# Wide tiles read as four rows of 2048 bytes instead of 2112 in an encoder block on one core

## The chip, the core and the metric

The kernel runs on one core of a Trainium2 chip. A core has five engines that each work through a stream of instructions of their own: TensorE (PE: matmuls; PEld: the loads of its stationary operand), VectorE (DVE), ScalarE (ACT), GpSimd (POOL) and SyncE (SP), with 16 DMA engines beside them. Its on-chip memory has 128 partitions, and matmul results land in eight PSUM banks of 128 x 512 f32. The metric is the device time of one execution in microseconds (us); lower is better.

## The reference

One layer of an encoder, f32, 512 positions of width 1024: a SwiGLU block, a mixer (a gated convolution beside a bidirectional chunked mLSTM with four heads), and a second SwiGLU block, each between two RMS norms.

```python
def swiglu(x, w_in, w_out):                   # w_in 1024 x 5632, w_out 2816 x 1024
    gate, up = jnp.split(x @ w_in, 2, axis=-1)
    return (jax.nn.silu(gate) * up) @ w_out
...
        h = swiglu(rmsnorm(x, norm_ffn1_pre[l]), w_ffn1_in[l], w_ffn1_out[l])
        x = x + FFN_RESIDUAL_SCALE * rmsnorm(h, norm_ffn1_post[l])
        h = mixer(rmsnorm(x, norm_mix_pre[l]), w_mix_in[l], conv_w[l], conv_b[l],
                  gate_i_bias[l], gate_f_bias[l], mlstm_norm[l], w_mix_out[l])
        x = x + rmsnorm(h, norm_mix_post[l])
        h = swiglu(rmsnorm(x, norm_ffn2_pre[l]), w_ffn2_in[l], w_ffn2_out[l])
        x = x + FFN_RESIDUAL_SCALE * rmsnorm(h, norm_ffn2_post[l])
```

## The kernel before

**Products in two halves.** Each large product is made of fp32r operands. `split` (L362) takes an f32 tile and makes `hi`, its fp32r copy (ScalarE, L363), and `lo`, the remainder (VectorE, L366). A product then is three matmuls or three runs of matmuls into one PSUM bank: hi times hi, hi times lo, lo times hi. Weights are read from HBM into `raw` tiles, split into `whi` and `wlo`, and most products are arranged as seven products of half-size blocks instead of eight (`combine_x`, `w_pair`, `left_a`, `left_b`, `product_out`), whose sums and differences VectorE forms.

**Wide tiles.** The pool `big` has 13 buffers of 128 partitions x 4 rows x `BW` = 528 numbers, that is 8448 bytes of a partition, in rows 2112 bytes apart. Nearly all users fill 512 numbers (2048 bytes) of a row and leave 64 bytes. Two users fill rows of 528: the weights of v with their 16 columns of gates behind 512 columns (`v_split`, L892), and `vaug` (L935), which holds v for four heads of 132 numbers a row. The others are the following.

- The normed and transposed input of a product, `xq_tile` (L402): one tile of hi and one of lo for each group of four rows of 128 features. These are the moving operands of `mm_cols` (L507, whole rows of 512 columns), of `mm_part` (L516, halves of a row, 256 columns), and of `plain` (L542, the same).
- `h`, the result of the first product of a SwiGLU block (L527), six tiles, a row for each 128 hidden features.
- `hs` (L767): in rows q and q+1 the hi and the lo of a row of `h`. They are the stationary operand of `mm_out` (L745), in blocks of 128 columns.
- `ea`, `eb`, `xb` (L706): intermediate sums of 512 columns.
- In the mixer: keys, queries, gates, convolution results, and the result tiles whose blocks are the stationary operand of the output projection (L1425); `RA`, `RB`, `HLT`, `QT` (L966 to L982) for the log-gate sums.
- As one flat run, not as rows: `halves` (L583), whose 256- or 512-wide pieces are the operands of `product_out` (L723), and the output weights of the mixer, `wmo` (L1407). Their pieces start at multiples of 512 bytes from the tile's start.

The innermost loops of the two forms that read rows as moving operands are these:

```python
        for ww, xx in ((0, "h"), (0, "l"), (1, "h")):
            for k in range(KD):
                nc.tensor.matmul(
                    o, w[ww][:, k, :], xq_tile(xq, (k // 4, xx))[:, k % 4, FULL], start=n == 0, stop=n == 3 * KD - 1)
...
        for ww, xx in ((hi, 0), (hi, 1), (lo, 0)):
            for k in range(4):
                pin(nc.tensor.matmul(
                    o, ww[:, k, :], x[xx][:, k, :], start=first and n == 0, stop=n == 11, skip_group_check=True))
```

**Stages.** The program runs, in us of the profiled execution: loads and first norm (0 to 26), the first product of the first SwiGLU block (26 to 257, L542 and L516), its second product (257 to 320, L723 and L745) and the norm behind it (to 344), the product for v and the gates (344 to 370, L950), the mixer (370 to 505, L507 and the recurrence), its output projection (505 to 548, L1425), and the second SwiGLU block in the same stages (548 to 858), with the last norms and the stores (to 887).

**Order.** A scheduler orders the instructions of each engine; instructions that pass through `pin` keep the order in which the code issues them, and `tc.issue_after` puts others behind a marked one. The big weights come over SP's DMA queue, some of them over POOL's. A tile of the pool `big` is given to a new user when its last reader is done.

Of the kernel before, what the change touches and what calls it, by code (L numbers as in the profile page):

```python
# [8 lines left out]
F32 = mybir.dt.float32  # L9
F32R = mybir.dt.float32r  # L10
# [6 lines left out]
P = 128  # L17
# [19 lines left out]
BW = 528  # L37
# [4 lines left out]
def encoder_kernel(ctx: ExitStack, tc: tile.TileContext, a: dict, out: bass.AP):  # L42
# [4 lines left out]
    big = ctx.enter_context(tc.tile_pool(name="big", bufs=13))  # L47
# [11 lines left out]
    def nm(s):  # L59
        uid[0] += 1  # L60
        return f"{s}_{uid[0]}"

    def bigt(dt=F32):
        return big.tile([P, 4, BW], dt, tag="big", name=nm("big"))

    def ps():
        return psum.tile([P, 512], F32, tag="ps", name=nm("ps"))
# [10 lines left out]
    def f32(ap):  # L78
        return ap.bitcast(F32)

    def blk(i, n=P):
        return slice(i * n, (i + 1) * n)

    def ch(v):
        return v.rearrange("p (c t) -> p c t", t=P)
# [211 lines left out]
    def w_get(ahead=2):  # L297
        w_split(max(0, 1 + ahead - len(ready)))
        return ready.pop(0)
# [62 lines left out]
    def split(hi, lo, src, eng=nc.vector):  # L362
        latest["hi"] = nc.scalar.copy(out=hi, in_=src)  # L363
        if pinned["act"]:
            pin(latest["hi"])
        latest["lo"] = eng.tensor_tensor(out=lo, in0=src, in1=f32(hi), op=ALU.subtract)  # L366
        pin(latest["lo"])
# [34 lines left out]
    def xq_tile(xq, key):  # L402
        if key not in xq["q"]:
            xq["q"][key] = bigt(F32R)
        return xq["q"][key]
# [7 lines left out]
    def flip_q(tb, xs, xq, halves=(0, 1), bank=None):  # L413

        full = []
        for b in halves:
            pt = bank or ps()
            for k in range(4):
                pin(nc.tensor.transpose(out=pt[:, blk(k)], in_=xs[:, blk(4 * b + k)], identity=ident))  # L419
            hi, lo = xq_hl(xq, (b, tb // 2))  # L420
            split(hi[:, :, blk(tb % 2)], lo[:, :, blk(tb % 2)], ch(pt))
            if b not in xq["f"]:
                xq["f"][b] = bigt()
            if bank:
                return lambda fn: pin(fn(xq["f"][b][:, :, blk(tb)], ch(pt)))
            full.append((b, pt))
        for b, pt in full:
            pin(nc.scalar.copy(xq["f"][b][:, :, blk(tb)], ch(pt)))
# [91 lines left out]
    def ffn(xq, between, finish, mid=None, within=None, ahead=(2, 2, 1, 1), late=None, prep=None, block=0):  # L520
# [4 lines left out]


        h = [bigt() for _ in range((NF + 3) // 4)]  # L527
        spare.extend(h[-1][:, q, 0:512] for q in (2, 3))

# [362 lines left out]
    def v_split():  # L892
        for i in range(4):
            if not loaded:
                w_load(1)
            (raw,), _ = loaded.pop(0)
            bt = bigt(F32R).rearrange("p q f -> p (q f)")
            hi, lo = (bt[:, blk(n, 2 * BW)].rearrange("p (k f) -> p k f", k=2) for n in range(2))
            split(hi[:, :, 0:512], lo[:, :, 0:512], raw.rearrange("p (k f) -> p k f", k=2))
            rg = rawg[:, 2 * i:2 * i + 2, :]  # L900
            nc.gpsimd.tensor_copy(out=hi[:, :, 512:BW], in_=rg)
            nc.gpsimd.tensor_tensor(out=lo[:, :, 512:BW], in0=rg, in1=f32(hi[:, :, 512:BW]), op=ALU.subtract)
            wv.append((hi, lo))
# [14 lines left out]
    def within1(tb):  # L918
        if tb >= 2:
# [6 lines left out]
            (2, 1): lambda: flip_q(2, st1[2], xT1), (3, 0): lambda: mark.update(latest), (3, 1): lambda: flip_q(3, st1[3], xT1),  # L926
        },
        finish1, wgates, within1, (1, 1, 1, 0), late1, v_split)
    xq = st["xq"]

# [1 line left out]
        return xq_hl(xq, (k // 4, tb // 2))[hl][:, k % 4, blk(tb % 2)]  # L932


    vaug = bigt()  # L935
    vv = vaug.rearrange("p c (h e) -> p c h e", e=BW // 4)
    nc.gpsimd.memset(vv[:, :, :, DV:DV + 1], 1.0)
    spread = t2()
# [26 lines left out]
    with tc.issue_after(mark["pow"].ins):  # L965
        RA, RB = bigt(), bigt()  # L966
        nc.gpsimd.memset(RA[0:36, 0:2], 0.0)
        I, F = RA[0:36, 0, 0:512], RA[0:36, 1, 0:512]
        T1, T2 = RA[0:36, 2, 0:512], RA[0:36, 3, 0:512]
        B, A = RB[0:36, 0, 0:512], RB[0:36, 1, 0:512]  # L970
        CM, U = RB[0:36, 2, 0:512], RB[0:36, 3, 0:512]
        nc.gpsimd.memset(U, 1.0)
        nc.gpsimd.memset(ch(U)[:, :, 0:1], 0.0)
        HLT = bigt(F32R)
        UHL, IHL = HLT[:, 0, 0:512], HLT[:, 1, 0:512]
        nc.gpsimd.memset(f32(HLT[:, 0:2]), 0.0)
        sel = HLT.rearrange("p q f -> p (q f)")[:, 2 * BW:2 * BW + 8 * P].rearrange("p (j m) -> p j m", m=P)
        QT = bigt()
        Q1, Q2 = QT[:, 0, 0:512], QT[0:36, 1, 0:512]
        nc.gpsimd.memset(QT[:, 0:2], 0.0)  # L980
        parl = QT[0:36, 2, 0:2 * DK]
        nc.gpsimd.tensor_copy(parl.rearrange("p (e x) -> p e x", x=DK), par.broadcast_to([36, 2, DK]))  # L982
        gm = const.tile([36, 4, 8], F32, name="gm")
        amax, gsum, mprev, aco = gm[:, 0, 0:4], gm[:, 1, 0:4], gm[:, 2, :], gm[:, 3, 0:4]
        nc.vector.memset(mprev[:, 0:1], NEG)
# [261 lines left out]
        pn2[:, 256:272], parl, acd.rearrange("p q c -> p (q c)"),  # L1247
        start=True, stop=True,
    )
    Ct = bigt()  # L1250
    Cf = Ct.rearrange("p q f -> p (q f)")
    Cs = Cf[:, 0:12 * 129].rearrange("p (q i e) -> p q i e", q=4, i=3)
    nat1 = Cf[:, 1552:2064].rearrange("p (c r) -> p c r", r=P)
# [147 lines left out]
    for n, k in enumerate(MIXK):  # L1401
        if n < 5:
            wmo[k] = w_get(0)
        else:
            raw = rawp.tile([P, 1024], F32, tag="raw", name=nm("raw"))
            nc.sync.dma_start(raw, wo[blk(k), :])
            bt = bigt(F32R).rearrange("p q f -> p (q f)")  # L1407
            split(bt[:, 0:1024], bt[:, 1024:2048], raw)
            wmo[k] = (bt[:, 0:1024], bt[:, 1024:2048])
    for tb in range(NT):  # L1410
# [58 lines left out]
```

## Time and profile before

| | |
|---|---|
| time, median of 3 runs | 888.0 us (886.79 to 888.97) |
| the profiled execution | 888.25 us |
| its span | 886.5 us |
| mean granted TensorE clock | 0.999 |
| PE busy | 875.6 us, 99% of the span, 6039 instructions |
| PEld busy | 807.4 us, 91% |
| DVE busy | 731.8 us, 83%, 1159 instructions |
| ACT busy | 491.8 us, 55%, 855 instructions |
| POOL busy | 93.7 us, 11%, 123 instructions |
| DMA | 123.24 MB, 139 GB/s over the span |

The span runs from the first to the last instruction that the profiler recorded; the execution takes 1.75 us more. Matmuls overlap in the pipeline, so their single durations (280 ns for a 128x256 one of L516) add up to more than their time, and the distance from one matmul to the next is the better measure. A row of the groups reads: line, engine, operation, result<-operands by the program's names, shapes, count, then busy time in us, mean ns of one, and the engine's idle time ahead of them with what ended it. A row of the chain reads: start and length in us, engine, tile, line and count of a piece in which the instructions follow each other on one engine. A row of the windows reads: the stretch, its length, then the busy time and count of each engine, the granted clock, the DMA engines' mean share and the GB/s moved.

### The profile page before, as it was taken

Reading aid. Unit: us, or ns where it says so; the run is one execution under the profiler, and the core shown is the slowest. Engines: PE = TensorE matmul, PEld = TensorE weight load, DVE = VectorE, ACT = ScalarE, POOL = GpSimd, SP = SyncE. Lnnn points to the kernel's source line nnn. Section 1 sums busy time; section 2 is a strip of 40 time slices with the busy share of each in tenths; the row PEclk is TensorE's granted clock in tenths of the full one; section 3 lists DMA queues with packets and bytes.
Section 4 is the critical chain, followed back from the end, with each engine's and each line's share of the span. In section 5 each row is a group of like instructions: output and inputs, shape, how many; then the busy total and the mean of one; then the engine's idle time right before and its main releaser. Section 6 shows DMA issues by size and latency. Waiting matters only on the chain.

```text
span 886.5 us, 15403 instructions
## 1 busy us (share of the span) xinstructions
PE 875.6 (99%) x6039; PEld 807.4 (91%) x6039; DVE 731.8 (83%) x1159; ACT 491.8 (55%) x855; POOL 93.7 (11%) x123
## 2 busy tenths in 40 slices
PE   8999999999999999999999999999999999999997
PEld 6999999999988889988988888999999999988885
DVE  6989898988889978887588757898898988869956
ACT  7656455544656645755565535654555555546722
POOL 5000000001132022100121011000000000223000
PEclk9999999999999999999999999999999999999999
DMA  8444433424998852442062733433333423899722
GB/s 255 126 120 121 118 94 98 118 84 129 216 261 201 278 181 83 121 118 71 1 190 91 213 111 102 128 105 108 96 96 96 132 83 105 201 243 231 267 72 95
DMA packets 140384, 123.24 MB, mean 139 GB/s; under 512 B 5500, under 2 KB 116112, under 8 KB 140312
## 3 DMA queue, kind: packets, MB, share of 16 engines
q1 hardware_dynamic: 129936, 97.62, 36.8%
q0 software_dynamic: 10368, 24.65, 12.5%
q8 instruction: 47, 0.77, 0.3%
q14 instruction: 25, 0.20, 0.1%
q10 hardware_dynamic: 8, 0.01, 0.0%
HBM read 115.96 MB, written 6.29 MB: 138 GB/s over the span
## 4 chain that ended last, share of the span: by engine, by line
PE 96%; DMA 1%; DVE 1%; issue 0%; ACT 0%; DVEq 0%; POOLq 0%; POOL 0%; ACTq 0%
PE ps L516 47%; PE ps L723 19%; PE ps L507 9%; PE ps L542 5%; PE ps L1425 5%; PE ps L745 5%; PE ps L950 3%; DMA raw<-in_w_mix_in_dram 1%; PE ps L419 1%; PE ps L1328 1%; DMA g_row<-in_norm_ffn_pre_dram 1%; PE ps L472 0%; PE ps L1336 0%; PE ps L1277 0%; DVE t L464 0%
## 5 line engine op out<-in xcount | busy, mean ns | idle before, releaser
L516 PE MATMUL ps<-big,whi 128*128 128x256 f32 x2064 | 283.8, 280 | 0.4 <-DVE t L1086 0.4
L516 PEld LDWEIGHTS ps<-big,whi 128*128 128x128 f32 x2064 | 261.0, 188 | 1.9 <-DVE t L1086 0.8
L363 ACT CAST whi<-raw 128x1024 fp32r<-128x1024 f32 x170 | 175.5, 1051 | 72.6 <-DVE raw L216 23.6
L366 DVE TENSOR_TENSOR wlo<-raw,whi 128x1024 fp32r<-128x1024 f32 x166 | 201.3, 1220 | 13.0 <-ACT whi L363 8.7
L516 PE MATMUL ps<-big,wlo 128*128 128x256 f32 x1032 | 161.6, 280 | 0.0
L516 PEld LDWEIGHTS ps<-big,wlo 128*128 128x128 f32 x1032 | 138.8, 188 | 0.0
L723 PE MATMUL ps<-whi,big 128*128 128x512 f32 x336 | 105.7, 389 | 0.0
L723 PEld LDWEIGHTS ps<-whi,big 128*128 128x128 f32 x336 | 62.9, 188 | 13.0
L516 PE MATMUL ps<-big,ws 128*128 128x256 f32 x516 | 69.9, 280 | 0.0
L170 POOL DMA_DIRECT2D raw<-in_w_ffn_out_dram x18 | 22.0, 1221 | 440.6 <-DMA raw<-in_w_ffn_out_dram 222.5
L723 PE MATMUL ps<-wlo,big 128*128 128x512 f32 x168 | 64.8, 389 | 0.0
L516 PEld LDWEIGHTS ps<-big,ws 128*128 128x128 f32 x516 | 64.7, 188 | 0.0
L690 ACT COPY t<-ps 128x256 f32<-128x256 f32 x40 | 14.9, 373 | 88.4 <-PE ps L516 88.4
L507 PE MATMUL ps<-big,whi 128*128 128x512 f32 x224 | 55.2, 397 | 0.0
L507 PEld LDWEIGHTS ps<-big,whi 128*128 128x128 f32 x224 | 41.4, 188 | 9.3
L363 ACT CAST whi<-t 128x1024 fp32r<-128x1024 f32 (+1 forms) x44 | 39.5, 913 | 15.3 <-DVE t L216 10.2
L366 DVE TENSOR_TENSOR wlo<-t,whi 128x1024 fp32r<-128x1024 f32 (+1 forms) x44 | 46.2, 1051 | 1.4 <-ACT whi L363 0.7
L745 PE MATMUL ps<-whi,big 128*128 128x512 f32 x128 | 40.3, 393 | 0.0
L723 PEld LDWEIGHTS ps<-wlo,big 128*128 128x128 f32 x168 | 31.5, 188 | 6.5
L692 DVE TENSOR_TENSOR t<-ps,t 128x256 f32<-128x256 f32 x40 | 16.9, 423 | 20.7 <-PE ps L516 20.5
L542 PE MATMUL ps<-big,whi 128*128 128x256 f32 x256 | 33.8, 283 | 0.0
L542 PEld LDWEIGHTS ps<-big,whi 128*128 128x128 f32 x256 | 31.7, 188 | 0.6 <-ACT big L363 0.3
(245 smaller groups left out, 1408.0 us busy)
## 6 DMA issues: line engine op xcount, KB each, us to landing
raw<-in_w_ffn_in_dram SPq DMA_DIRECT2D x68, 512.0 KB, 4.6
raw<-in_w_ffn_out_dram SPq DMA_DIRECT2D x26, 512.0 KB, 4.7
raw<-in_w_mix_in_dram SPq DMA_DIRECT2D x24, 512.0 KB, 4.7
t<-in_w_ffn_in_dram SPq DMA_DIRECT2D x20, 512.0 KB, 3.7
raw<-in_w_ffn_out_dram SPq DMA_DIRECT2D x36, 256.0 KB, 6.2
raw<-in_w_ffn_out_dram POOLq DMA_DIRECT2D x18, 512.0 KB, 7.8
xd<-x POOLq DMA_DIRECT2D x8, 512.0 KB, 2.9
x<-xd POOLq DMA_DIRECT2D x8, 512.0 KB, 5.2
```

What stands on the lines that cost most here:

```text
L170: nc.gpsimd.dma_start(sums.rearrange("p (g f) -> p g f", g=2), top[:, 512:1024].rearrange("p (g f) -> p g f", g=1).broadcast_to([P, 2, 512 ...
L363: latest["hi"] = nc.scalar.copy(out=hi, in_=src)
L366: latest["lo"] = eng.tensor_tensor(out=lo, in0=src, in1=f32(hi), op=ALU.subtract)
L507: nc.tensor.matmul(o, w[ww][:, k, :], xq_tile(xq, (k // 4, xx))[:, k % 4, FULL], start=n == 0, stop=n == 3 * KD - 1)
L516: pin(nc.tensor.matmul(o, ww[:, k, :], x[xx][:, k, :], start=first and n == 0, stop=n == 11, skip_group_check=True))
L542: pin(nc.tensor.matmul(o, ww[:, k, :], xq_hl(xq, (k // 4, th))[xx][:, k % 4, :], start=n == 0, stop=n == 3 * KD - 1))
L690: nc.scalar.copy(a_[:, h1], x[:, h0])
L692: nc.vector.tensor_tensor(out=c[:, h1], in0=y[:, h0], in1=a_[:, h1], op=ALU.add)
L723: nc.tensor.matmul(acc[tb + t][half], left[n][x][:, blk(t)], right[n][y], start=first and x == y == 0, stop=last_ and x == 1, skip_group_c ...
L745: nc.tensor.matmul(acc[tb][half], hT[hh][:, blk(tb)], w[ww][:, blk(half, 512)], start=fresh and hh == ww == 0, stop=k == NF - 1 and hh == ...
L950: nc.tensor.matmul(pv_[i][:, 0:at.stop - at.start], xv(xx, k, tb), ww[:, k % 2, at], start=n == 0, stop=n == 3 * KD - 1)
L1425: nc.tensor.matmul(acc[half], yy[yi][:, k % 4, blk(tb)], wmo[k][wi][:, blk(half, 512)], start=(n == 0 and yi == 0 and wi == 0), stop=(n == ...
```

## The change

A new helper `wide()` makes the tile as it was, 128 x 2112 numbers. `bigt()` now takes its first 2048 numbers and reads them as four rows of 512, so that rows lie 2048 bytes apart. Where a row needs 528 numbers (`v_split`, `vaug`), or where the tile is used flat past 2048 numbers (`Ct`), the tile is taken from `wide()` as before; `wmo` takes it flat. `sel` starts at the number 8 x 128 = 1024 of `HLT` instead of 2 x 528 = 1056: the start of the third row, as before. The pool, its 13 buffers and their size stay.

```diff
+    def wide(dt=F32):
+        return big.tile([P, 4 * BW], dt, tag="big", name=nm("big"))
+
     def bigt(dt=F32):
-        return big.tile([P, 4, BW], dt, tag="big", name=nm("big"))
+        return wide(dt)[:, 0:2048].rearrange("p (q f) -> p q f", q=4)
...
-            bt = bigt(F32R).rearrange("p q f -> p (q f)")
+            bt = wide(F32R)
             hi, lo = (bt[:, blk(n, 2 * BW)].rearrange("p (k f) -> p k f", k=2) for n in range(2))
...
-    vaug = bigt()
+    vaug = wide().rearrange("p (q f) -> p q f", q=4)
...
         HLT = bigt(F32R)
         UHL, IHL = HLT[:, 0, 0:512], HLT[:, 1, 0:512]
         nc.gpsimd.memset(f32(HLT[:, 0:2]), 0.0)
-        sel = HLT.rearrange("p q f -> p (q f)")[:, 2 * BW:2 * BW + 8 * P].rearrange("p (j m) -> p j m", m=P)
+        sel = HLT.rearrange("p q f -> p (q f)")[:, 8 * P:16 * P].rearrange("p (j m) -> p j m", m=P)
...
-    Ct = bigt()
+    Ct = wide().rearrange("p (q f) -> p q f", q=4)
...
-            bt = bigt(F32R).rearrange("p q f -> p (q f)")
+            bt = wide(F32R)
             split(bt[:, 0:1024], bt[:, 1024:2048], raw)
```

On every engine the instructions are the same in kind, number, order and waits before and after; only addresses differ, and the length of three memsets on POOL, at the place in the mixer where the tiles of the log-gate sums are cleared (`big_4357` is `RA`, `big_4358` is `RB`, `big_4362` is `HLT`, `big_4364` is `QT`). POOL's rows there before:

```order
L967 MEMSET big_4357 36x1056
L972 MEMSET big_4358 36x512
L976 MEMSET big_4362 128x1056
L980 MEMSET big_4364 128x1056
L982 COPY big_4364<-par 36x128
L973 MEMSET big_4358 36x4
```

and POOL's rows there with the change (its lines are three further on):

```order
L970 MEMSET big_4357 36x1024
L975 MEMSET big_4358 36x512
L979 MEMSET big_4362 128x1024
L983 MEMSET big_4364 128x1024
L985 COPY big_4364<-par 36x128
L976 MEMSET big_4358 36x4
```

Nothing has moved; the three memsets over two whole rows no longer cover the 64 bytes at the end of each row.

## The prediction

> **What bounds the kernel now.** I read first the chain of work that ended last, then what TensorE waits for, then the busy time by stage, and last the chain again piece by piece, because a piece of it has a start, a length and a count, and so gives the spacing of the matmuls in it.
>
> ```profile
> span 886.5 us, 15403 instructions
> PE 96%; DMA 1%; DVE 1%; issue 0%; ACT 0%; DVEq 0%; POOLq 0%; POOL 0%; ACTq 0%
> PE ps L419 <- DVE t L464: 2.8, 2, 2.3
> PE ps L353 <- POOL gbias L877: 1.4, 1, 1.4
> PE ps L516 <- DVE t L1086: 0.4, 1, 0.4
> ```
>
> TensorE is 96% of the chain, and in the whole execution it waits 4.6 us for another engine. So almost all of the time is matmuls that stand directly behind each other, and a change counts only through the spacing of matmuls. The stages say how much cover the other engines have:
>
> ```profile
> core 0: us, PE busy (x) PEld busy (x) DVE busy (x) ACT busy (x) POOL busy (x), PEclk, DMA share, GB/s
> 26.00:257.00 231.00, 231.00 (x1873) 227.09 (x1872) 202.80 (x312) 126.56 (x200) 12.88 (x12) 1.00 0.48 130
> 344.00:370.00 26.00, 26.00 (x219) 25.96 (x217) 19.58 (x30) 17.99 (x40) 7.12 (x12) 1.00 0.33 104
> 575.00:796.00 221.00, 221.00 (x1783) 216.84 (x1782) 188.31 (x298) 117.01 (x190) 12.09 (x11) 1.00 0.47 126
> ```
>
> In the two long stretches of 256-wide products VectorE is busy 202.80 of 231 us and 188.31 of 221 us, the DMA engines about half of the time. TensorE can gain some 10% there before another engine is the bound. The granted clock is 1.00 in all three stages, so nothing here hangs on the clock.
>
> **What one matmul costs, by where its operands lie.** The pieces of the chain below are start, length, line and count. Each length divided by its count is the spacing from one matmul to the next.
>
> ```profile
> 37.41 196.29 PE ps L516 x1668
> 237.87 83.00 PE ps L723 x366
> 376.67 27.34 PE ps L507 x118
> 504.14 22.27 PE ps L1425 x96
> 858.13 22.09 PE ps L745 x96
> ```
>
> The last four are all 128x512 matmuls of the same type, yet their spacings are 83.00/366 = 226.8 ns (L723), 27.34/118 = 231.7 (L507), 22.27/96 = 232.0 (L1425) and 22.09/96 = 230.1 (L745). Not even the order within them explains it: L723, L745 and L1425 all take left and right operands in the order hi-hi, hi-lo, lo-hi. What sets L723 apart is its addresses. In the built program the wide tiles start at 24256 + n x 8448 bytes of a partition and the weight tiles at 134080 + n x 4096, and all of these starts lie 192 bytes past a multiple of 256. L723 reads weight tiles and flat halves of wide tiles, in steps of 512, 1024, 2048 and 4096 bytes, so every operand of it keeps that place. L507 streams rows of wide tiles 2112 bytes apart, and 2112 = 8 x 256 + 64: each row begins 64 bytes further on in the 256-byte period. L745 and L1425 load their stationary operand from such rows. With rows of 2048 = 8 x 256 bytes all of them would lie as L723's do. That is the one thing in the profile which this change can move.
>
> The durations of single matmuls say the same as the spacings:
>
> ```profile
> L723 PE MATMUL ps<-whi,big 128*128 128x512 f32 x336 | 105.7, 389 | 0.0
> L507 PE MATMUL ps<-big,whi 128*128 128x512 f32 x224 | 55.2, 397 | 0.0
> L745 PE MATMUL ps<-whi,big 128*128 128x512 f32 x128 | 40.3, 393 | 0.0
> L1425 PE MATMUL ps<-whi,big 128*128 128x512 f32 x80 | 26.4, 394 | 0.0
> L1425 PE MATMUL ps<-big,big 128*128 128x512 f32 x72 | 18.8, 396 | 0.0
> ```
>
> 389 ns stands for L723 in every group, 393 to 397 for the others.
>
> **The change part by part.** The order of instructions, their number and their waits stay as they were on every engine.
>
> *512-wide matmuls.* L507 runs 336 times, L745 192 times, L1425 192 times. If they take L723's spacing, they save 336 x (231.7 - 226.8) = 1.65 us, 192 x (230.1 - 226.8) = 0.63 us and 192 x (232.0 - 226.8) = 1.00 us, together **3.3 us**. All of it is on the chain: these pieces are TensorE behind TensorE. Bounds: nothing, if the addresses are not the cause, and 3.3 us; I take the full 3.3, since L723 is the only group with this layout and holds its spacing over 366 matmuls.
>
> *256-wide matmuls whose moving operand is a wide row.* L516 runs 3612 times and L542 384 times, 3996 together, so each nanosecond of spacing is 4.0 us: this is the large unknown. Now they stand at 196.29/1668 = 117.7 ns, with each moving row 64 bytes further on than the one before. The trace has no 256-wide matmul of this type in the layout to come. The nearest rows:
>
> ```profile
> 106.77 1.22 PE L516 MATMUL ps<-big,ws 128*128 128x256 f32 x9
> 107.83 1.57 PE L516 MATMUL ps<-big,whi 128*128 128x256 f32 x12
> 109.24 0.63 PE L516 MATMUL ps<-big,wlo 128*128 128x256 f32 x4
> ...
> 111.70 0.64 PE L516 MATMUL ps<-big,wlo 128*128 128x256 f32 x4
> 112.18 0.98 PE L516 MATMUL ps<-big,whi 128*128 128x256 f32 x7
> ```
> ```profile
> 344.80 8.75 PE ps L950 x72
> ```
>
> From below: the same saving as at 512 columns, 4.9 ns, gives 112.8 ns and 3996 x 4.9 = 19.6 us. If the saving goes with the columns, it is half of that, 2.45 ns and 9.8 us. From above: runs of four in L516 take between (109.24 - 107.83)/12 = 117.5 ns and (112.18 - 111.70)/4 = 120.0 ns, the slow ones where the scheduler has put another product in between and the 64-byte step is broken; if the slow spacing became the rule, the loss were 2.3 ns and 9.2 us. The nearest row is L950: it runs pairs of 256 and 272 columns over one weight, the second of each pair 1024 bytes after the first, thus with no step in the 256-byte period. Its mean is 8.75/72 = 121.5 ns for a mean of 264 columns; taking off 8 columns at (231.7 - 117.7)/256 = 0.445 ns leaves 117.9 ns, against 117.7 with the step. So I take **0** for the 256-wide matmuls, and keep -19.6 and +9.2 us as ends.
>
> A page of the Trainium skill speaks against any effect: TensorE: Matmul & The Clock Gate, section Back-to-back issue gap, gives the gap of a warm matmul as its columns over 2.4 GHz plus about 2.5 ns, with no address in it. By that rule 512 columns take 215.8 ns and 256 take 109.2 whatever the pitch, and the change is worth nothing. The rows agree only in part: the same shape stands at four spacings here, all of them above the rule's.
>
> *VectorE and ScalarE.* They read and write the same rows, in one to four runs.
>
> ```profile
> L366 DVE TENSOR_TENSOR wlo<-raw,whi 128x1024 fp32r<-128x1024 f32 x166 | 201.3, 1220 | 13.0 <-ACT whi L363 8.7 <-PE ps L723 3.0 <-ACT junk L1362 0.8
> L366 DVE TENSOR_TENSOR big<-t,big 128x1024 fp32r<-128x1024 f32 x6 | 7.3, 1222 | 0.0
> L428 ACT COPY big<-ps 128x512 f32<-128x512 f32 x12 | 6.9, 589 | 2.3 <-DVE big L366 2.1
> L479 ACT COPY raw<-ps 128x512 f32<-128x512 f32 x4 | 2.4, 589 | 2.3 <-DVE big L366 2.2
> ```
>
> A subtraction over one flat run takes 1220 ns, over four runs 2112 bytes apart 1222; a copy into runs 2112 apart takes 589 ns, into runs 1024 apart 589. The pitch costs these engines nothing that can be seen, so I put 0 there, between bounds of plus and minus 2 ns an instruction; even 2 ns on all of them lies under TensorE.
>
> *The three memsets on GpSimd*, which clear two whole rows each, shrink from 1056 to 1024 numbers.
>
> ```profile
> L967 POOL MEMSET big<- 36x1056 f32 x1 | 1.0, 972 | 0.0
> L972 POOL MEMSET big<- 36x512 f32 x1 | 0.5, 517 | 0.0
> ```
>
> That is (972 - 517)/544 = 0.84 ns a number, 27 ns each, 0.08 us in all, on an engine that is busy 7.12 of 26 us in that stage (344 to 370) and that TensorE is not waiting for. It counts 0. The DMAs into wide rows move 512 numbers to a partition before and after.
>
> **The sum.** The profiled execution took 888.25 us, 1.75 us of it around the span of 886.5; it lies 0.25 us above the median of 888.0 of the runs shown. 888.25 - 3.3 = 884.95 for it, and against the median 888.0 - 3.3 = **884.7 us**.
>
> **The rivals.**
>
> *Nothing changes: 888.0 us.* For it: L723 has no fixed spacing either. Its first twelve matmuls, with the same addresses to the 256 bytes, are slow:
>
> ```profile
> 233.70 2.76 PE ps L723 x12
> ```
>
> 2.76/12 = 230.0 ns, as slow as L745. So the slow spacing also comes from something that is not the address, perhaps the change from 256-wide to 512-wide products just before, and L507, L745 and L1425 may be slow for such a reason. Against it: L745 runs 96 in a row at 858.13 without ever becoming fast, L723 becomes fast after its first dozen and stays so.
>
> *The 256-wide matmuls gain too.* Then 888.0 - 3.3 - 9.8 = 874.9 us if the gain goes with the columns, and 888.0 - 3.3 - 19.6 = 865.1 us if each matmul gains the same. For it: their moving rows step by 64 bytes just as L507's do. Against it: L950's spacing above. No other engine would cap it: 1680 matmuls at 4.9 ns take 8.2 us from the stretch of 231 us and leave 222.8, above VectorE's 202.80.
>
> *The 256-wide matmuls lose: slower than before.* The mechanism is the one place: a matmul whose moving row starts at the same place of the 256-byte period as the one before it. In L516 that happens now only where products are interleaved, and runs of four there take up to 120.0 ns. If every one of the 3996 took 120.0 ns, the kernel would take 888.0 - 3.3 + 9.2 = 893.9 us. It decides from 3.3/3996 = 0.8 ns on; from 1.5 ns on the kernel is slower by more than 0.3%. For it: at 512 columns the good layout still costs 226.8 ns where twice 112.8 would be 225.6, so a part of the cost is fixed for each matmul and may be larger than I take it. Against it: L950.
>
> **How the numbers follow.** Chances: my forecast, 512-wide gain alone and the 256-wide within 0.8 ns either way (881.5 to 888), 0.36; nothing changes (887 to 889) 0.22; 256-wide gain (865 to 881.5) 0.24; 256-wide lose (888 to 894) 0.18. About 0.3%, 2.7 us, is what a measurement of this kernel can tell from no change: faster means under 885.3, slower over 890.7. Of the forecast's 0.36, 0.23 lies under 885.3 and 0.13 above. Faster is then 0.23 + 0.24 = 0.47; of the losing case's 0.18, 0.04 lies under 890.7. Same is 0.13 + 0.22 + 0.04 = 0.39, less 0.01 for a case of no change that comes out above 890.7 by the spread of the runs, thus 0.38; slower is 0.14 + 0.01 = 0.15. The range of 8 in 10 leaves out the lower half of the gaining case, 0.12, and the upper end of the losing one, 0.05: **869 to 892 us**. The likeliest case's own range is 881.5 to 888.
>
> **What would show it.** In the profile of the changed kernel, right: the chain's pieces of L507, L745 and L1425 at 226.8 ns, single durations of 389 ns in place of 393 to 397, and L516 at 117.7 +- 0.8 ns over its run of about 1668. VectorE and ScalarE groups keep their means. Wrong: L507 still at 231.7 (then the addresses are not the cause, and L723 is fast for its own reasons), or L516 away from 117.7, which decides the time alone, since 4.0 us hang on each of its nanoseconds. A new wait of TensorE for VectorE in the stretch 26 to 257 would mean that I have misjudged the cover.

## The result and the profile after

The changed kernel takes 893.55 us (median of 6 runs, 892.69 to 894.2) against 887.45 us before (6 runs, 886.79 to 888.97): a ratio of 1.0065, 95% interval 1.0055 to 1.0076. It is 0.65% slower, clear of what a measurement can confuse with no change. The forecast was 884.7 us, the range 869 to 892.

The head of the page of the changed kernel, whose lines are numbered three higher than before:

```profile
span 891.6 us, 15403 instructions
PE 882.6 (99%) x6039; PEld 817.1 (92%) x6039; DVE 731.6 (82%) x1159; ACT 492.2 (55%) x855; POOL 92.2 (10%) x123
```

The span is 5.1 us longer, VectorE and ScalarE are about as busy as before (731.8 and 491.8 there), and TensorE's busy time grew by 7.0 us, while its waits fell by 1.9 us, from 4.6 to the 2.7 shown below. Next the pieces of the changed kernel's chain that answer to those of before (start, length, line, count):

```profile
37.32 200.16 PE ps L519 x1668
241.66 82.99 PE ps L726 x366
380.07 26.78 PE ps L510 x118
506.09 21.79 PE ps L1428 x96
577.67 197.28 PE ps L519 x1644
863.58 21.77 PE ps L748 x96
```

Each piece has the count that it had before, so lengths compare directly. The 512-wide products became faster: `mm_cols` (L510) from 27.34 to 26.78 us, which is 226.9 ns a matmul, the output projection (L1428) from 22.27 to 21.79, 227.0 ns, `mm_out` (L748) from 22.09 to 21.77, 226.8 ns; `product_out` (L726) kept its spacing, 226.8 before and 226.7 now. The 256-wide product `mm_part` (L519) became slower: 196.29 to 200.16 us for 1668 matmuls, 117.7 to 120.0 ns.

What TensorE waits for in the changed kernel, whole answer (engine, line, releaser: us in total, times, longest):

```profile
PE ps L356 <- POOL gbias L880: 1.4, 1, 1.4
PE ps L422 <- DVE t L467: 1.3, 2, 1.1
```

No wait in a product took the place of another: both are in the start of the program. What changed in the products is the spacing of matmuls. 3996 x 2.32 ns = 9.3 us lost, and 336 x 4.75 + 192 x 3.3 + 192 x 5.0 ns = 3.2 us gained, is 6.1 us, the difference of the two medians.

### The profile page after: what moved, and what is told of

It reads as the page before. It is cut to its first block, busy times and chain, and to the rows that moved or that the text cites. A ratio compares the mean times of both kernels' runs of the same rounds, so it can differ in the third digit from the quotient of the medians.

```text
span 891.6 us, 15403 instructions
## 1 busy us (share of the span) xinstructions
PE 882.6 (99%) x6039; PEld 817.1 (92%) x6039; DVE 731.6 (82%) x1159; ACT 492.2 (55%) x855; POOL 92.2 (10%) x123
## 4 chain that ended last, share of the span: by engine, by line
PE 98%; DMA 1%; DVE 0%; ACT 0%; issue 0%; DVEq 0%; POOLq 0%; POOL 0%; SPq 0%; ACTq 0%
PE ps L519 49%; PE ps L726 19%; PE ps L510 9%; PE ps L545 5%; PE ps L1428 5%; PE ps L748 5%; PE ps L953 3%; PE ps L1331 1%; PE ps L422 1%; DMA x<-in_x_dram 1%; PE ps L1339 0%; PE ps L475 0%; PE ps L1280 0%; PE ps L1307 0%; PE ps L1300 0%; PE ps L1373 0%
## 5 line engine op out<-in xcount | busy, mean ns | idle before, releaser
L519 PE MATMUL ps<-big,whi 128*128 128x256 f32 x2064 | 288.6, 283 | 0.0
L519 PEld LDWEIGHTS ps<-big,whi 128*128 128x128 f32 x2064 | 266.2, 192 | 1.1 <-ACT t L1312 0.2
L519 PE MATMUL ps<-big,wlo 128*128 128x256 f32 x1032 | 164.2, 283 | 0.0
L519 PEld LDWEIGHTS ps<-big,wlo 128*128 128x128 f32 x1032 | 141.7, 192 | 0.0
L726 PE MATMUL ps<-whi,big 128*128 128x512 f32 x336 | 105.6, 389 | 0.0
L726 PEld LDWEIGHTS ps<-whi,big 128*128 128x128 f32 x336 | 62.9, 188 | 12.9
L519 PE MATMUL ps<-big,ws 128*128 128x256 f32 x516 | 71.2, 283 | 0.0
L519 PEld LDWEIGHTS ps<-big,ws 128*128 128x128 f32 x516 | 66.0, 192 | 0.0
L726 PE MATMUL ps<-wlo,big 128*128 128x512 f32 x168 | 64.7, 389 | 0.0
L510 PE MATMUL ps<-big,whi 128*128 128x512 f32 x224 | 54.5, 394 | 0.0
L510 PEld LDWEIGHTS ps<-big,whi 128*128 128x128 f32 x224 | 41.4, 188 | 8.7
L748 PE MATMUL ps<-whi,big 128*128 128x512 f32 x128 | 39.8, 390 | 0.0
L726 PEld LDWEIGHTS ps<-wlo,big 128*128 128x128 f32 x168 | 31.6, 188 | 6.5
L545 PE MATMUL ps<-big,whi 128*128 128x256 f32 x256 | 34.2, 285 | 0.0
L545 PEld LDWEIGHTS ps<-big,whi 128*128 128x128 f32 x256 | 32.1, 192 | 0.5 <-ACT big L366 0.3
```

Source lines behind the costliest of these rows:

```text
L510: nc.tensor.matmul(o, w[ww][:, k, :], xq_tile(xq, (k // 4, xx))[:, k % 4, FULL], start=n == 0, stop=n == 3 * KD - 1)
L519: pin(nc.tensor.matmul(o, ww[:, k, :], x[xx][:, k, :], start=first and n == 0, stop=n == 11, skip_group_check=True))
L545: pin(nc.tensor.matmul(o, ww[:, k, :], xq_hl(xq, (k // 4, th))[xx][:, k % 4, :], start=n == 0, stop=n == 3 * KD - 1))
L726: nc.tensor.matmul(acc[tb + t][half], left[n][x][:, blk(t)], right[n][y], start=first and x == y == 0, stop=last_ and x == 1, skip_group_c ...
L748: nc.tensor.matmul(acc[tb][half], hT[hh][:, blk(tb)], w[ww][:, blk(half, 512)], start=fresh and hh == ww == 0, stop=k == NF - 1 and hh == ...
```

## The experiments

Two theories could be had from the result. **The step:** the rival of the prediction, by which a matmul is slow at 256 columns when its moving row starts at the same place of the 256-byte period as the row before it. **The relative place:** what counts is how far the moving row's start lies from the stationary block's start modulo 256 bytes; in the changed kernel both are at byte 192 throughout, whereas before, rows 2112 bytes apart went through all four distances 0, 64, 128 and 192. A third, **the traffic of other engines** at the new pitch, had to be excluded. In the following, *distance* is the start of the moving row less the start of the stationary block, modulo 256 bytes, from the built programs. All matmuls named below have fp32r operands and a stationary block of 128 x 128, and TensorE runs the same 6039 instructions in the same order in every kernel here.

### Moving rows alone back to 2112 bytes (x_2112)

```diff
-    def bigt(dt=F32):
-        return wide(dt)[:, 0:2048].rearrange("p (q f) -> p q f", q=4)
+    def bigt(dt=F32, pitch=512):
+        return wide(dt)[:, 0:4 * pitch].rearrange("p (q f) -> p q f", q=4)
...
-            xq["q"][key] = bigt(F32R)
+            xq["q"][key] = bigt(F32R, 528)
```

> Only the moving rows (the tiles that xq_tile makes, for both SwiGLU blocks and the mixer) go back to rows 2112 bytes apart; all other wide tiles keep 2048. Theory, the step: the spacing of matmuls hangs on whether the moving row starts at the same place of the 256-byte period as the one before it. Then mm_part returns from 120.0 to 117.6 ns, mm_cols from 227 to 231.7, while mm_out and the output projection, whose stationary rows stay at 2048, keep 226.8 and 227.0: 893.55 - 3996 x 2.32 ns + 336 x 4.7 ns = 885.9 us. Rival, the traffic of the other engines: the loss comes from VectorE, ScalarE and DMAs that read and write the wide rows at another pitch while TensorE streams; since most of these rows (h, hs, ea, eb, xb) stay at 2048, mm_part would stay near 120 ns and the time near 893.

Measured: 885.83 us (one run; before on the same chip 887.09). Its chain:

```profile
36.19 196.29 PE ps L519 x1668
375.06 27.34 PE ps L510 x118
502.89 21.79 PE ps L1428 x96
856.02 21.77 PE ps L748 x96
```

The first two pieces have the lengths of the kernel before to the hundredth, the last two those of the changed one. So the pitch of the moving rows sets `mm_part` and `mm_cols`, the pitch of the stationary rows sets `mm_out` and the projection, and the other engines' traffic in `h`, `hs`, `ea`, `eb` and `xb` sets neither. The traffic rival falls for these tiles. What the other engines write into the moving rows themselves went back to the old pitch too; gap64 below, with every row at 2048 bytes, excludes that as well. The step theory and the relative place both fit.

### Only the rows read in halves back to 2112 (x_mix)

With the helper of x_2112:

```diff
-            xq["q"][key] = bigt(F32R)
+            xq["q"][key] = bigt(F32R, 512 if "m" in xq and isinstance(key, tuple) else 528)
```

> Moving rows that are read in halves of 256 columns go back to 2112 bytes (both SwiGLU blocks, and the four tiles of differences in the mixer); the mixer's tiles that are read over 512 columns, and all rows that serve as stationary operand, keep 2048. By the step theory mm_part and plain take 117.6 ns (but for some 108 matmuls of the mixer that share the 512-wide tiles), mm_cols, mm_out and the output projection 226.8 to 227: 893.55 - 3888 x 2.32 ns = 884.5 us, thus under the kernel before (887.45) by 0.3%. By the rival of the other engines' traffic it stays near 893.

Measured: 884.59 us (8 runs) against 887.09, ratio 0.9975 (0.9965 to 0.9986). From its chain:

```profile
36.66 196.29 PE ps L519 x1668
375.56 26.78 PE ps L510 x118
```

`mm_part` has the spacing of the kernel before and `mm_cols` that of the changed one, so the two terms are separate. The time is 2.5 us under the kernel before, where the prediction had forecast 3.3 for the 512-wide term by itself; some 108 matmuls of 256 columns, in the mixer, still had the slow layout here, which by 2.32 ns each is 0.25 us of the rest.

### A step of 32 bytes (x_2080)

Also with the helper of x_2112:

```diff
-            xq["q"][key] = bigt(F32R)
+            xq["q"][key] = bigt(F32R, 520)
```

> All moving rows 2080 bytes apart: a step of 32 bytes instead of 64. If any break of the place in the period counts, mm_part takes 117 to 118 ns and mm_cols 230 to 232: 885.9 us, as with 2112. If the size of the step sets the gain in proportion, mm_part takes 118.8 ns and the time is some 889.7. If only whole 64-byte blocks count, mm_part stays at 120.0 and mm_cols at 227: 893.5.

Measured: 888.93 us (one run; before 887.09). From its chain:

```profile
36.32 197.65 PE ps L519 x1668
376.62 27.24 PE ps L510 x118
```

`mm_part` takes 118.5 ns, `mm_cols` 230.8: between the two layouts, near the line for a gain in proportion (118.8 ns, 889.7 us). By itself this told little. A step of 32 bytes also goes through the four distances 0, 32, 64 and 96 instead of 0, 64, 128 and 192, which is another mean under the second theory.

### Distance 192 without a step (gap64)

```diff
+    gapw = ctx.enter_context(tc.tile_pool(name="gapw", bufs=1))
     wpool = ctx.enter_context(tc.tile_pool(name="wpool", bufs=12))
...
+    gapw.tile([P, 16], F32, name="gapw")
```

> All rows at 2048 as in the changed kernel, but the weight tiles (and the tiles behind them) start 64 bytes later, so that moving rows start at byte 192 and the stationary blocks of mm_part at byte 0 of the 256-byte period, throughout and without any step. Step theory: nothing changes, mm_part 120.0 ns and 893.5 us. Rival, the relative place: the slow spacing comes from both operands starting at the same place of the period, which before happened for a quarter of the matmuls only; then mm_part falls to 117 ns or less, 884 us or less, and mm_out and the output projection leave 226.8.

Measured: 873.42 us (one run; before 887.09). From its chain, whose lines are two higher than the changed kernel's:

```profile
37.33 189.04 PE ps L521 x1668
230.50 83.77 PE ps L728 x366
369.97 27.53 PE ps L512 x118
843.40 21.99 PE ps L750 x96
```

All rows are 2048 bytes apart, there is no step anywhere, and `mm_part` takes 189.04/1668 = 113.3 ns instead of 120.0. The step theory falls: it had said 120.0. At the same time every 512-wide product left its best: `mm_cols` at distance 192 takes 233.3 ns, `product_out` and `mm_out` at distance 64 take 228.9 and 229.1. The sum 3996 x -6.7 + 336 x 6.4 + 756 x 2.2 + 384 x some 2.5 ns is -22.0 us; measured are -20.1. Of the rest, 1.0 us is a wait of the first product for ScalarE, which the changed kernel does not have; the remainder is not worked out.

### The same distance by moving the other operand (at48)

```diff
-    def bigt(dt=F32):
-        return wide(dt)[:, 0:2048].rearrange("p (q f) -> p q f", q=4)
+    def bigt(dt=F32, at=0):
+        return wide(dt)[:, at:at + 2048].rearrange("p (q f) -> p q f", q=4)
...
-            xq["q"][key] = bigt(F32R)
+            xq["q"][key] = bigt(F32R, 0 if "m" in xq and isinstance(key, tuple) else 48)
```

> Weight tiles stay where the changed kernel has them (byte 192 of the 256-byte period). The moving rows that are read in halves of 256 columns start 48 numbers (192 bytes) further into their wide tile, rows 2048 bytes apart: byte 128, thus again 192 bytes behind the stationary blocks modulo 256, as in gap64, but by moving the other operand. The mixer's tiles that are read over 512 columns, and all stationary rows, stay at byte 192, in step with what they meet. Theory, the relative place: mm_part and plain take 113.4 ns, mm_cols 227, mm_out 226.8, product_out 226.8: 893.55 - 3888 x 6.55 ns = 868.1 us, if VectorE keeps up (it was busy 183 of 200 us in the first long stretch of gap64). Rival, the absolute place of the weights (gap64 was fast because the weight tiles began at byte 0): mm_part stays at 120.0 ns, 893.5 us.

Measured: 868.83 us (median of 6 runs, five of them from 868.43 to 869.32 and one of 876.38, for which no cause is known) against 887.22, ratio 0.9809 (0.9783 to 0.9835). Its chain, then what TensorE waits for:

```profile
36.05 189.04 PE ps L519 x1668
229.24 82.96 PE ps L726 x366
367.63 26.78 PE ps L510 x118
564.68 186.32 PE ps L519 x1644
839.52 21.77 PE ps L748 x96
```

```profile
PE ps L356 <- POOL gbias L880: 1.4, 1, 1.4
PE ps L422 <- DVE t L467: 0.9, 2, 0.5
PE ps L519 <- DVE t L1089: 0.8, 1, 0.8
```

The weights are where the changed kernel has them, and `mm_part` takes the 189.04 us of gap64 all the same: the place of the weights alone is not the cause; the distance is what the two kernels share. The 512-wide products keep distance 0 and their best spacing, so this kernel has both gains; it is the fastest of the study, 1.9% under the kernel before and 2.8% under the changed one. VectorE keeps up, as the only wait for it in a product is 0.8 us long.

### Both operands moved together (all0)

```diff
+    gapb = ctx.enter_context(tc.tile_pool(name="gapb", bufs=1))
     big = ctx.enter_context(tc.tile_pool(name="big", bufs=13))
...
+    gapb.tile([P, 16], F32, name="gapb")
```

> The changed kernel with 64 bytes put in ahead of the wide tiles, so that wide tiles and weight tiles both start at byte 0 of the period and their distance is 0 as in the changed kernel. Relative place: mm_part 120.0, mm_cols 227, mm_out 226.8, 893.5 us. Absolute place of either operand: mm_part leaves 120.0, and comes to 113.4 if gap64 was fast through the weights at byte 0.

Measured: 893.85 us (one run; before 887.22). From its chain:

```profile
37.20 200.16 PE ps L521 x1668
241.54 83.22 PE ps L728 x366
380.16 26.80 PE ps L512 x118
863.92 21.77 PE ps L750 x96
```

In `mm_part`, `mm_cols` and `mm_out` both operands start 64 bytes further on, at byte 0, and their pieces are the changed kernel's: 120.0, 227.1 and 226.8 ns. Moving both operands by 64 bytes makes no difference as long as their distance stays. `product_out` alone became slower, 83.22 us against 82.99. 168 of its 756 stationary blocks lie in the tiles `xl`, in a pool ahead of the added 64 bytes, which did not move; their distance is now 64 instead of 0, and a matmul with such a block lasts 391 to 392 ns in this trace, one with another block 389. In gap64, with distance 64 throughout, all of them last 391 to 392 ns.

### The other distances (at16, at32, at40, at56)

The edit is that of at48 with other numbers: 16, 32, 40 and 56 numbers for the rows read in halves, and 32, 48, 8 and 56 for the mixer's rows read over 512 columns.

> As at48, but the rows read in halves start 64 bytes into their tile (64 ahead of the stationary blocks modulo 256) and the mixer's rows read over 512 columns 128 bytes (128 ahead). Relative place: if only the equal place is bad at 256 columns, mm_part takes 113.4 ns and the time is 868 to 870; if the spacing changes with the distance, anything from 113.4 to 123 (the pitch 2080 showed single intervals of up to 124). mm_cols over 512 columns leaves 227 for 229 to 234. Absolute place of the weights: 120.0 and 893.5.

> As at16, with 128 bytes for the rows read in halves and 192 bytes for the mixer's rows read over 512 columns. Relative place: mm_cols takes 233.3 ns, as in gap64 at the same distance; mm_part somewhere between 113.4 and 123, 113.4 if only the equal place is bad. Absolute place of the weights: 120.0 and 227.

> A finer look at the distance: rows read in halves 160 bytes into their tile, the mixer's rows read over 512 columns 32 bytes. The spacings so far over the distance: at 256 columns 120.0 (0), 117.8 (64), 118.7 (128), 113.5 ns (192); at 512 columns 227 (0), 229 (64), 232.6 (128), 233.3 (192). If the spacing moves evenly between these points, mm_part takes 116.1 ns and mm_cols 228: 878.8 us. If only the whole 64-byte block of the start counts, 160 acts as 128 and 32 as 0: mm_part 118.7, mm_cols 227, 889 us; if it is rounded up, 113.5 and 229, 869.5 us.

> Rows read in halves and the mixer's rows read over 512 columns both 224 bytes into their tile. Evenly between the points: mm_part 116.7 ns, mm_cols 230, 882 us. By whole 64-byte blocks: as at 192, mm_part 113.5, mm_cols 233.3, 870.9 us. If the best place lies between 192 and 256: mm_part under 113.4 and the time under 868.

Measured: 886.24 and 889.14 us (one run each, before 887.22) for at16 and at32; 889.53 us (ratio 1.0021, 1.0011 to 1.0031) for at40 and 888.62 us (1.0013, 1.0003 to 1.0022) for at56, both against 887.36. The two pieces of each chain, in this order of kernels:

```profile
36.80 196.45 PE ps L519 x1668
375.84 27.42 PE ps L510 x118
```

```profile
36.41 197.94 PE ps L519 x1668
376.97 27.53 PE ps L510 x118
```

```profile
36.84 197.94 PE ps L519 x1668
377.63 27.54 PE ps L510 x118
```

```profile
37.47 197.38 PE ps L519 x1668
377.67 27.54 PE ps L510 x118
```

Length by count, with the kernels above, gives the spacing over the distance (an empty place was not measured):

| distance, bytes | 256 columns (`mm_part`), ns | 512 columns, ns |
|---|---|---|
| 0 | 120.0 (after, all0) | 226.9 (`mm_cols`, after) |
| 32 | | 233.4 (at40) |
| 64 | 117.8 (at16) | 228.9 (`product_out`, gap64) |
| 128 | 118.7 (at32) | 232.4 (at16) |
| 160 | 118.7 (at40) | |
| 192 | 113.3 (gap64, at48) | 233.3 (gap64, at32) |
| 224 | 118.3 (at56) | 233.4 (at56) |

Neither of the guesses between the points held. An even course would have given 116.1 and 116.7 ns at 160 and 224 bytes for 256 columns, where 118.7 and 118.3 came; for 512 columns, 32 bytes is slower than both of its neighbours. Counting by whole blocks of 64 bytes, from the start of a block, was right at 160 bytes for 256 columns (118.7, as at 128) and at 224 for 512 (233.4, 233.3 at 192), but wrong at 224 for 256 columns and at 32 for 512. At either width one distance stands out as good, 0 for 512 columns and 192 for 256. The distance that is best for one is the worst, or within 0.1 ns of the worst, for the other. That multiples of 256 bytes don't count at distances 0, 64 and 192 is seen from the piece of 1668 matmuls: the wide tiles lie 33 x 256 bytes apart and the weight tiles 16 x 256, so it goes through many of them, yet the starts of its matmuls give 120.0 ns as the mean of every twelve in the changed kernel, 117.8 in at16, and 113.2 to 113.4 in gap64 and at48. At 128, 160 and 224 bytes the means of twelve spread over 0.8 to 0.9 ns, so something besides this distance may count there.

## Why the prediction was wrong

**The bound was right.** TensorE's matmuls behind each other are the time, in every kernel here, and the cover was judged rightly: at 113.3 ns VectorE still keeps up, as the waits of at48 show.

**The 512-wide term was right, with its cause not quite.** Forecast were 3.3 us, measured 3.2, and the spacings came out as L723's: 226.8 to 227.0 ns. The prediction said that L723 is special because every operand "keeps that place". What counts is that both operands have the same place: in gap64 every operand of `product_out` keeps its place too, but the distance is 64, and it takes 228.9 ns. The rival "nothing changes" leaned on the first twelve matmuls of L723; they take 2.75 us in the changed kernel, 2.76 before, so what makes that short piece slow was not what made the long ones slow.

**The step that failed is the value for the 256-wide matmuls:** "So I take **0** for the 256-wide matmuls". Measured is +2.32 ns on each of 3996, 9.3 us. The value came from L950, taken as the nearest row because it had "no step in the 256-byte period". The quantity was the wrong one. What would have had to be compared is the distance between a matmul's own two operands, and L950 has distance 0 in half of its matmuls and 128 in the other half, with 272 columns in every second one; it says nothing of 256 columns at distance 0 throughout. Nor is the spacing of before, 117.7 ns, that of one distance. It is close to the mean of the four distances through which rows 2112 bytes apart go: (120.0 + 117.8 + 118.7 + 113.3)/4 = 117.45 ns. For 512 columns the mean is (226.9 + 228.9 + 232.4 + 233.3)/4 = 230.4, against 231.7 in `mm_cols`, 230.1 in `mm_out` and 232.0 in the projection. That the spacing of before is this mean is argued from its size, not shown: by the starts in its trace, the four rows of a group stand at 117.5, 117.9, 117.5 and 117.8 ns, not at the four values. What is shown is that a pitch of 2048 holds one distance, here the best one for 512 columns and the worst one for 256.

**The losing rival had the price and not the mechanism.** It gave 893.9 us from the 120.0 ns of the interleaved runs, and 893.55 came. But its reason, a moving row at the place of the one before it, holds in gap64 and at48 as well, which run at 113.3. And the price came by luck: it divides by four the difference of two starts in hundredths of a us, 0.48, so it is uncertain by some 2.5 ns, and the starts in ns are 473 apart, 118.3 ns a matmul. The rival had a chance of 0.18 and one price, 893.9, above the 892.0 at which the range ended: the range cut off a case at the very number that the case gave.

**The rule of the page,** which has no address in it (the Trainium skill, TensorE: Matmul & The Clock Gate, section Back-to-back issue gap), had spoken for no change. The section gives it for an isolated matmul, and says that in a stream of weight loads and matmuls, as here, both set the spacing. The runs do not bear the formula out here: the same 256-wide matmul takes 113.3 to 120.0 ns by address alone, where the formula gives 109.2, at a granted clock of 0.998 in the changed kernel and in at48.

**VectorE, ScalarE and GpSimd** behaved as forecast. The subtraction over a flat run and a cleared tile of the changed kernel:

```profile
L369 DVE TENSOR_TENSOR wlo<-raw,whi 128x1024 fp32r<-128x1024 f32 x166 | 201.0, 1218 | 12.2 <-ACT whi L366 8.0 <-PE ps L726 3.0 <-ACT junk L1365 1.0
L970 POOL MEMSET big<- 36x1024 f32 x1 | 0.9, 942 | 0.0
```

The first took 1220 ns before; the memset lost 30 ns of 972, where 27 were forecast, and nobody waits for it.

**What stays open:** why the distance matters, and why 0 is good at 512 columns and bad at 256. In the changed kernel the weight loads are busy for 92% of the span and the matmuls for 99%, so the two run at the same time; whether their reads get into each other's way, no run here looks into. Nor do the runs tell whether the block that counts is the matmul's own or the next one, since they lie at the same place modulo 256 in `mm_part`. Distances that aren't multiples of 32 bytes weren't tried.

## What to carry to other kernels

Where TensorE is the bound, note for each group of matmuls the start of its moving row and of its stationary block modulo 256 bytes, and divide the chain's pieces by their counts: among the round pitches here, a spacing belonged to a distance and a width. A row pitch that is no multiple of 256 goes through several distances, which here was better for 256 columns than the wrong one held fixed, so moving to a round pitch needs the distance chosen with it, for each width apart. Here an offset of 192 bytes in the tiles of the 256-wide rows was worth 24.7 us (893.55 to 868.83), with the pool as large as before. Only fp32r operands were tried.

## What was not expected of the hardware

The size of it: 6.7 ns of 120.0, 5.6%, between two placements of the same 256-wide fp32r matmul, and 6.5 ns of 226.9 at 512 columns. And how narrow the good places are: 32 bytes to either side of 192 cost 5.0 to 5.4 ns at 256 columns, 32 bytes from 0 cost 6.5 ns at 512.
